# A float32 decoder trunk on one core: plain products for one K-tile pair in four, a two-pass up projection over two blocks at once, and operand work queued in stages

## The chip, the core and the metric

One core of a Trainium2 chip. The metric is the device time of the whole program in microseconds (us), the median of several runs; lower is better.

## The reference, cut to what matters

Two pre-norm residual layers over 256 tokens of width 2048, all in float32. Each layer has a mixer (attention of several kinds between an input and an output projection) and then a squared-ReLU MLP with 8192 hidden columns. The change lies in the MLP.

```
def squared_relu_mlp(h, w_up, w_down):
    return jnp.square(jax.nn.relu(h @ w_up)) @ w_down

for layer in range(2):
    x = x + mixer(rms_norm(x, attn_norm[layer]))
    h = rms_norm(x, mlp_norm[layer])
    x = x + squared_relu_mlp(h, w_up[layer], w_down[layer])
return rms_norm(x, final_norm)
```

## The kernel before, in words

**Three passes for a float32 product.** Each operand is split in two parts of a narrower format: `hi`, the rounded value, which ScalarE writes, and `lo`, the rest, which VectorE gets by a subtraction. A product is then hi·hi + hi·lo + lo·hi. The activations are kept as one tile `xs` per K-tile with the hi columns 0 to 255 and the lo columns 256 to 511; the weights are split as they arrive.

**The stream.** The program is one list, `stream`, of pairs (block, chunk). A block is a set of output columns with its accumulators in PSUM; a chunk is a piece of K, four K-tiles of 128 rows by 256 columns, one `hi` and one `lo` tile of 128x1024. Two or four chunks share a *unit*, 1 MB of weights in a `raw` tile, of which there are three; SyncE loads them in order, each as soon as the last reader of the `raw` tile three units back is done. The loop at the end of `trunk` does for every i: the `hi` tiles up to chunk i+4 (L1265), the `lo` tiles up to chunk i+3 (L1273), then the matmuls of chunk i, and what a finished block needs. Every engine works through its own instructions in this written order. `jobs.tick()` after some chunks takes the next step of the spawned jobs: each job is a generator, and what stands between two of its `yield` lines is written at one place.

**The MLP.** The 8192 hidden columns are eight groups of 1024. In a group the *up* blocks (kind "U", four of 256 hidden columns, four chunks each) make h = relu(x·w_up)^2. The chunks are here called U0 to U15. For each K-tile and 128 columns there are three matmuls of 256 columns (L466 to L468), the first two with the same weights. A finished block (`up_done`) is read from PSUM by ScalarE's Relu (L1003) and squared (L1005), and a job then makes the operands of the next step from the squares `hr`: four additions on VectorE (L1014 to L1017), the hi part on ScalarE (L1018), the lo part on VectorE (L1019).

The *down* projection of groups 0 to 6 uses a product scheme that replaces eight block products of a 2x2 split by seven (kind "S"): four column blocks (`cb`) of 512 columns, each with two units of two K-tile pairs. A unit has four chunks: `plain` (two panels), `single` (one panel), and two whose weights are made on VectorE first, `w13` by L1046 and `w24` by L1052 and L1053. The seven sums of a column block lie in PSUM tiles `s0` and `s1`, are copied out by ScalarE (L1075) and added up in DRAM by GpSimd's accumulating DMAs (L1080). After group 6 `combine` puts the seven sums together in DRAM with seven more accumulating DMAs (L1092) and loads the result (L1096).

Group 0's up chunks stand alone. Then the list has, for each later group, two S chunks of the group before, one up chunk, and so on: `plain`, `single`, U, `w13`, `w24`, U. One *period* is one S unit and two up chunks; a group has eight. The last group's down projection (eight blocks of kind "U") follows, and takes the combined sums in by matmuls with the identity (L1106, `add_sums`).

PSUM: the up blocks have two tiles of one bank each; `s0` and `s1` have two banks each; a separate pool keeps two banks for small side work (`side()`).

## Time and profile before

| | |
|---|---|
| median of 3 runs | 2212.97 us (2207.54 to 2217.98) |
| the profiled execution | 2218.0 us; its span is 2216.2 us |
| TensorE matmul busy | 2160.6 us (97%), 16390 matmuls |
| VectorE busy | 1707.8 us (77%) |
| ScalarE busy | 1297.2 us (59%) |
| DMA | 459.75 MB, mean 207 GB/s |

"Busy" counts an engine as busy while any of its instructions runs, and matmuls overlap each other, so TensorE's 97% is no measure of its pace: the pace is read from the starts of matmuls. "L466" is line 466 of the kernel before; PE is TensorE, DVE VectorE, ACT ScalarE, POOL GpSimd, SPq SyncE's DMA queue. Released waits are written "waiter <- releaser".

### The profile page before, as it was taken

The numbers are of one execution on the slowest core, as the hardware profiler recorded it, in microseconds if no ns is written. First come the engines' busy times: TensorE is split into PE (matmuls) and PEld (weight loads), VectorE is DVE, ScalarE is ACT, GpSimd is POOL, SyncE is SP. The second block draws the span as 40 slices with busy tenths as digits, with TensorE's granted clock in tenths as the row PEclk, the third lists the DMA queues.
The fourth block names the chain that finished last, engine by engine and source line by source line (L and its number), as shares of the span: only waits on it lengthen the run. The fifth ranks groups of instructions, "written<-read, shape, count | busy, mean of one in ns | idle before, by whom it ended". The sixth has DMA issues, their size and how long they took to land.

```text
span 2216.2 us, 40047 instructions
## 1 busy us (share of the span) xinstructions
PE 2160.6 (97%) x16390; PEld 2071.6 (93%) x16390; DVE 1707.8 (77%) x2169; ACT 1297.2 (59%) x1746; POOL 170.7 (8%) x225
## 2 busy tenths in 40 slices
PE   9999999999999999998999999999999999999988
PEld 7898989999999999998988899899999999999987
DVE  6765666888889898886766665568888888889865
ACT  6554545576666666665555446455666666666552
POOL 0000000000000000013100000000000000000131
PEclk9999999999999999999999999999999999999999
DMA  8545456577888888899754455565778888888994
GB/s 261 175 148 162 153 183 179 187 242 222 234 230 233 232 229 234 224 243 263 211 171 141 155 173 179 149 191 178 243 216 237 226 232 232 224 237 232 243 262 135
DMA packets 306279, 459.75 MB, mean 207 GB/s; under 512 B 11992, under 2 KB 181024, under 8 KB 306096
## 3 DMA queue, kind: packets, MB, share of 16 engines
q1 hardware_dynamic: 280224, 392.32, 56.5%
q0 software_dynamic: 25840, 64.87, 14.9%
q8 instruction: 129, 2.11, 0.4%
q14 instruction: 54, 0.44, 0.1%
q10 hardware_dynamic: 32, 0.01, 0.0%
HBM read 403.68 MB, written 60.82 MB: 210 GB/s over the span
## 4 chain that ended last, share of the span: by engine, by line
PE 45%; DVE 17%; ACT 16%; DMA 13%; issue 9%; POOL 1%; ACTq 0%; SPq 0%; DVEq 0%; POOLq 0%
PE mm L475 14%; DVE lo L1273 9%; ACT hi L1265 8%; PE mm L476 8%; DMA raw<-w_up 7%; DVE w L1046 4%; PE up L468 3%; ACT stage L1075 3%; PE up L466 3%; DMA sums<-sums 3%; PE up L467 3%; PE mm L460 2%; DMA raw<-w_down 2%; PE mm L462 2%; PE mm L461 2%
## 5 line engine op out<-in xcount | busy, mean ns | idle before, releaser
L1273 DVE TENSOR_TENSOR lo<-raw,hi 128x1024 fp32r<-128x1024 f32 (+1 forms) x756 | 825.3, 1114 | 242.8 <-ACT hi L1265 83.7
L1265 ACT ACTIVATE hi<-raw 128x1024 fp32r<-128x1024 f32 (+1 forms) x756 | 717.7, 967 | 498.4 <-DMA raw<-w_up 232.9
L468 PE MATMUL up<-xs,lo 128*128 128x256 f32 x2048 | 583.1, 285 | 30.2 <-DVE lo L1273 29.8
L466 PE MATMUL up<-xs,hi 128*128 128x256 f32 x2048 | 580.3, 283 | 8.9 <-ACT hi L1265 7.3
L467 PE MATMUL up<-xs,hi 128*128 128x256 f32 x2048 | 580.2, 283 | 0.0
L499 PE MATMUL s<-hi,hs 128*128 128x256 f32 x1568 | 441.0, 281 | 0.0
L500 PE MATMUL s<-lo,hs 128*128 128x256 f32 x1568 | 440.2, 281 | 0.0
L501 PE MATMUL s<-hi,hs 128*128 128x256 f32 x1568 | 439.8, 280 | 0.0
L468 PEld LDWEIGHTS up<-xs,lo 128*128 128x128 f32 x2048 | 389.7, 190 | 41.6 <-DVE lo L1273 41.6
L466 PEld LDWEIGHTS up<-xs,hi 128*128 128x128 f32 x2048 | 386.8, 189 | 10.0 <-ACT hi L1265 10.0
L467 PEld LDWEIGHTS up<-xs,hi 128*128 128x128 f32 x2048 | 387.0, 189 | 0.0
L475 PE MATMUL mm<-xs,hi 128*128 128x512 f32 x885 | 319.5, 401 | 1.5 <-DVE t L1115 0.9
L1265 ACT ACTIVATE hi<-w 128x1024 fp32r<-128x1024 f32 x224 | 236.1, 1054 | 124.8 <-DVE w L1053 86.7
L500 PEld LDWEIGHTS s<-lo,hs 128*128 128x128 f32 x1568 | 296.0, 189 | 0.0
L499 PEld LDWEIGHTS s<-hi,hs 128*128 128x128 f32 x1568 | 295.6, 189 | 0.0
L501 PEld LDWEIGHTS s<-hi,hs 128*128 128x128 f32 x1568 | 295.4, 188 | 0.0
L1273 DVE TENSOR_TENSOR lo<-w,hi 128x1024 fp32r<-128x1024 f32 x224 | 273.8, 1222 | 21.5 <-ACT hi L1265 16.7
L476 PE MATMUL mm<-xs,lo 128*128 128x256 f32 x944 | 259.0, 279 | 0.2 <-DVE lo L1273 0.2
L475 PEld LDWEIGHTS mm<-xs,hi 128*128 128x128 f32 x885 | 166.0, 188 | 39.2 <-ACT hi L1265 1.1
L476 PEld LDWEIGHTS mm<-xs,lo 128*128 128x128 f32 x944 | 177.3, 188 | 3.0 <-DVE lo L1273 0.5
L1080 POOL DMA_DIRECT2D sums<-stage x96 | 86.6, 902 | 877.3 <-ACT stage L1075 865.7
L1046 DVE TENSOR_TENSOR w<-raw 128x1024 f32<-128x1024 f32 x112 | 136.7, 1220 | 0.0
(295 smaller groups left out, 2775.2 us busy)
## 6 DMA issues: line engine op xcount, KB each, us to landing
raw<-w_up SPq DMA_DIRECT2D x128, 1024.0 KB, 6.0
raw<-w_down SPq DMA_DIRECT2D x128, 1024.0 KB, 6.8
raw<-od_w_in SPq DMA_DIRECT2D x36, 1024.0 KB, 5.0
raw<-ev_w_in SPq DMA_DIRECT2D x30, 1024.0 KB, 5.3
sums<-stage POOLq DMA_DIRECT2D x56, 512.0 KB, 5.8
sums<-stage POOLq DMA_DIRECT2D x56, 384.0 KB, 6.5
raw<-ev_w_out SPq DMA_DIRECT2D x16, 1024.0 KB, 5.0
raw<-od_w_in SPq DMA_DIRECT2D x20, 512.0 KB, 4.7
```

The source lines that it names most:

```text
L466: mm(ps[:, j], hi[:, n, c], m[:, 0:T], start=first and j == 0, stop=False)
L467: mm(ps[:, j], hi[:, n, c], m[:, T:], start=False, stop=False)
L468: mm(ps[:, j], lo[:, n, c], m[:, 0:T], start=False, stop=last and j == 1)
L475: mm(ps[:, j], hi[:, n, c], m, start=first, stop=False)
L476: mm(ps[:, j, 0:T], lo[:, n, c], m[:, 0:T], start=False, stop=False)
L499: mm(ps, x[:, a, 0:P], hi[:, o, q], start=first and at % 2 == 0, stop=False)
L500: mm(ps, x[:, a, 0:P], lo[:, o, q], start=False, stop=False)
L501: mm(ps, x[:, a, P:], hi[:, o, q], start=False, stop=last and (at % 2 == 1 or prod == 3))
L1046: tt(four(t), w[:, :, :, 1].rearrange("p q k c -> p k q c"), w[:, :, 0].rearrange("p q h c -> p h q c"), op=OP.subtract)
L1080: nc.gpsimd.dma_start(to, stage, accum_op=OP.add)
L1265: act(d, r, AF.Copy)
L1273: tt(d, r, f32(h), op=OP.subtract)
```

## The change

1. **Up projection.** A block is now of kind "T", as in the mixers: for each K-tile and 128 columns one matmul of 512 columns (hi weights with hi and lo activations) and one of 256 (lo weights). The products hi·lo come out in PSUM columns of their own, so a block takes two tiles of two banks, and `up_done` becomes: ScalarE copies one half out, VectorE adds the other half to it, ScalarE does Relu and Square. Two blocks that share a 512-column load are worked through together, chunk by chunk: blocks 0 and 1 end at U6 and U7, blocks 2 and 3 at U14 and U15.
2. **One K-tile pair in four without products** (`PLAIN = (3,)`): for pair 3 the eight plain block products replace the seven. It needs no sums of weights and no four additions on `hr`. The sums become eight, in two equal halves of 128x1024; `combine` has one DMA more.
3. **Stages.** `w13` is made when the unit's first `hi` is written, `w24` at its second; the chunk order is `plain`, `single`, `w13`, `w24` as before. The job on `hr` has a `yield` after the additions and one after the hi part; its first step comes with the next tick for blocks 0 and 2 (`delay=b % 2`).
4. **PSUM.** The side pool is gone; in the mixers the side tiles come from the same pool as the other banks, in the MLP `side()` takes half of `s0` or `s1`.

```
@@ consume @@
-                mm(ps[:, j], hi[:, n, c], m[:, 0:T], start=first and j == 0, stop=False)
-                mm(ps[:, j], hi[:, n, c], m[:, T:], start=False, stop=False)
-                mm(ps[:, j], lo[:, n, c], m[:, 0:T], start=False, stop=last and j == 1)
+                o = ps[:, j, 0:T]
...
@@ mlp @@
+        PLAIN = (3,)
...
-        sums = [dram.tile([P, 7 * T], F32, name=f"sums{layer}_{cb}") for cb in range(4)]
+        sums = [dram.tile([P, 8 * T], F32, name=f"sums{layer}_{cb}") for cb in range(4)]
...
         def take_up():
-            return st["banks"].tile([P, 2, T], F32, name="up", bufs=2)
+            return banks("up", 2)
...
         def up_done(grp, b):
             def f(ps):
                 t = temp()
-                act(t, ps, AF.Relu)
+                act(t, ps[:, :, T:], AF.Copy)
+                tt(t, ps[:, :, 0:T], t, op=OP.add)
+                act(t, t, AF.Relu)
+                if (grp, b) != (0, 0):
+                    need(("h", layer) + (grp, b - 1) if b else ("h", layer, grp - 1, nb - 1))
...
+                    elif b in PLAIN:
+                        act(h[:, 0:4, 0:P], r[:, 0:4], AF.Copy)
+                        yield 1, 0
+                        tt(h[:, 0:4, P:], r[:, 0:4], f32(h[:, 0:4, 0:P]), op=OP.subtract)
                     else:
...
                         tt(r[:, 7], r[:, 3], r[:, 5], op=OP.subtract)
+                        yield 1, 0
                         act(h[:, :, 0:P], r[:, 1:8], AF.Copy)
+                        yield 1, 0
                         tt(h[:, :, P:], r[:, 1:8], f32(h[:, :, 0:P]), op=OP.subtract)
...
-                jobs.spawn(job(), keys=[("h", layer, grp, b)], delay=1)
+                jobs.spawn(job(), keys=[("h", layer, grp, b)], delay=b % 2)
...
@@ product_chunks @@
-                chunks += [Chunk(unit, ks, plain, prods=((X11, 1), (X12, 2))),
-                           Chunk(unit, ks, single, prods=((S4, 3),)),
-                           Chunk(unit, ks, of(13), prep13, ((S1, 5), (S3, 7))),
-                           Chunk(unit, ks, of(24), prep24, ((S2, 6), (X22, 4)))]
+                for q in range(2):
+                    if q in prod:
+                        one += [(2 * q, X11, prs[q], 1), (2 * q + 1, X12, prs[q], 2)]
+                    else:
+                        one += [(2 * q, 1, prs[q], 2), (2 * q + 1, 3, prs[q], 2),
+                                (2 * q, 0, prs[q], 4), (2 * q + 1, 2, prs[q], 4)]
...
+                chunks += [Chunk(unit, prs, views_of((4, column)), prep13 if nq else None, one),
+                           Chunk(unit, prs, views_of(*rest), prep24 if nq else None, two)]
...
@@ combine @@
-            for step in (((p2, p1), (p6, p1)), ((p7, p6),), ((p6, p5), (p4, p7)), ((p3, p6), (p7, p5))):
+            for step in (((p2, p1), (p6, p1)), ((p7, p6),), ((p6, p5), (p4, p7), (p8, p5)), ((p3, p6), (p7, p8))):
...
@@ up_list @@
-            blocks = [Block("U", eights(up, grp * W + b * T, KT), mov, up_done(grp, b), take=take_up)
-                      for b in range(nb)]
-            return [(block, i) for block in blocks for i in range(len(block.chunks))]
+            order = []
+            for b in range(0, nb, 2):
+                c = w_chunks(up, grp * W + b * T, fours(KT))
+                two = [Block("T", c[i], mov, up_done(grp, b + i), take=take_up) for i in range(2)]
+                order += [(block, i) for i in range(len(c[0])) for block in two]
+            return order
...
@@ hi_to @@
+            for d, r in views(i, his[i]):
+                act(d, r, AF.Copy)
             prep = stream[i][0].chunks[stream[i][1]].prep
             if prep:
                 prep()
-            for d, r in views(i, his[i]):
-                act(d, r, AF.Copy)
```

**Place 1: VectorE where an up block has ended.** Before, a block's last chunk is followed by two S chunks before the job's turn; `lo_6180` and `lo_6197` are those of `w13` and `w24`, `lo_6216` that of the up chunk behind them.

```order
L1273 TENSOR_TENSOR lo_6180<-w13_6142,hi_6141 128x1024
L1273 TENSOR_TENSOR lo_6197<-w24_6176,hi_6175 128x1024
L1014 TENSOR_TENSOR hr_6173<-hr_6173 128x128
L1015 TENSOR_TENSOR hr_6173<-hr_6173 128x128
L1016 TENSOR_TENSOR hr_6173<-hr_6173 128x128
L1017 TENSOR_TENSOR hr_6173<-hr_6173 128x128
L1019 TENSOR_TENSOR hs_6207<-hr_6173,hs_6207 128x7x128
L1273 TENSOR_TENSOR lo_6216<-raw_6065,hi_6195 128x1024
```

Now, at the end of block 2 of a group (chunk U14, tile `up_5407`); `lo_5762` is that of U15, `lo_5798` and `lo_5808` those of the next S unit's first and second chunk.

```order
L1318 TENSOR_TENSOR lo_5762<-raw_5622,hi_5734 128x1024
L1010 TENSOR_TENSOR t_5782<-up_5407,t_5782 128x512
L1028 TENSOR_TENSOR hr_5786<-hr_5786 128x128
L1029 TENSOR_TENSOR hr_5786<-hr_5786 128x128
L1030 TENSOR_TENSOR hr_5786<-hr_5786 128x128
L1031 TENSOR_TENSOR hr_5786<-hr_5786 128x128
L1067 TENSOR_TENSOR w24_5795<-w13_5760,raw_5636 128x512
L1068 TENSOR_TENSOR w24_5795<-raw_5636,w24_5795 128x512
L1318 TENSOR_TENSOR lo_5798<-raw_5636,hi_5758 128x1024
L1318 TENSOR_TENSOR lo_5808<-raw_5636,hi_5793 128x512
L1318 TENSOR_TENSOR lo_5822<-raw_5738,hi_5806 128x1024
```

The addition from PSUM (L1010) and the four on `hr` (L1028 to L1031) now stand between the `lo` of U15 and the next `lo`, with ScalarE's Relu and Square between L1010 and L1028. On TensorE the twelve matmuls of the unit's two `w` chunks and the sixteen of U15 stand between the end of `up_5407` and the first use of `lo_5798`. The lo part of `hs` (L1035) now comes later, after the next block's addition.

**Place 2: VectorE over one S unit, where the `raw` tile has its last reader.** Before (`raw_6080` is the unit, `raw_6199` the up unit beside it):

```order
L1273 TENSOR_TENSOR lo_6247<-raw_6080,hi_6214 128x1024
L1273 TENSOR_TENSOR lo_6264<-raw_6080,hi_6245 128x512
L1046 TENSOR_TENSOR w13_6279<-raw_6080 128x1024
L1273 TENSOR_TENSOR lo_6282<-raw_6199,hi_6262 128x1024
L1052 TENSOR_TENSOR w24_6309<-w13_6279,raw_6080 128x512
L1053 TENSOR_TENSOR w24_6309<-raw_6080,w24_6309 128x512
```

Now (`raw_5884` is the unit, `raw_5868` and `raw_5989` the up units before and beside it):

```order
L1059 TENSOR_TENSOR w13_6011<-raw_5884 128x1024
L1318 TENSOR_TENSOR lo_6013<-raw_5868,hi_5985 128x1024
L1067 TENSOR_TENSOR w24_6035<-w13_6011,raw_5884 128x512
L1068 TENSOR_TENSOR w24_6035<-raw_5884,w24_6035 128x512
L1318 TENSOR_TENSOR lo_6038<-raw_5884,hi_6009 128x1024
L1318 TENSOR_TENSOR lo_6048<-raw_5884,hi_6033 128x512
L1318 TENSOR_TENSOR lo_6061<-raw_5989,hi_6046 128x1024
```

The last reader of an S unit's `raw` tile was L1053, behind the `lo` of the up chunk beside it; it is now the second `lo` (here `lo_6048`), ahead of that up chunk's `lo`.

## Rows read from the trace of the kernel before

**Rows 1.** Windows, layer 0: stretch, its length, busy us (instructions) by engine, PEclk, DMA share, GB/s.
```profile
407.00:975.00 568.00, 555.77 (x4612) 550.90 (x4611) 503.20 (x584) 371.57 (x433) 42.47 (x52) 1.00 0.81 230
975.00:1038.00 63.00, 56.62 (x441) 55.57 (x441) 46.72 (x47) 37.42 (x45) 23.68 (x31) 0.95 0.97 250
```
**Rows 2.** Waits of PE, 407 to 975 us, then 1512 to 2090 us: total, times, longest.
```profile
PE up L468 <- DVE lo L1273: 12.1, 23, 1.2
...
PE up L468 <- DVE lo L1273: 13.9, 25, 1.4
```
**Rows 3.** The chain of waits, 583 to 612 us: start, us, what.
```profile
585.64 8.79 DMA raw<-w_up
...
595.60 1.23 DVE lo L1273
596.83 0.61 DVE w L1052
...
597.46 0.70 DVE w L1053
...
608.03 9.35 DMA raw<-w_up
```
**Rows 4.** Timeline of PE, single matmuls (up, then S): start us, us, what.
```profile
361.14 0.28 PE L466 MATMUL up<-xs,hi 128*128 128x256 f32 x1
...
445.47 0.28 PE L499 MATMUL s<-hi,hs 128*128 128x256 f32 x1
...
448.32 0.28 PE L466 MATMUL up<-xs,hi 128*128 128x256 f32 x1
...
1037.79 0.28 PE L466 MATMUL up<-hs,hi 128*128 128x256 f32 x1
...
1505.89 0.28 PE L466 MATMUL up<-xs,hi 128*128 128x256 f32 x1
...
1512.01 0.28 PE L466 MATMUL up<-xs,hi 128*128 128x256 f32 x1
```
**Rows 5.** Timeline of PE in the odd mixer, kind "T", six pairs apart.
```profile
1272.15 0.39 PE L475 MATMUL mm<-xs,hi 128*128 128x512 f32 x1
...
1274.25 0.39 PE L475 MATMUL mm<-xs,hi 128*128 128x512 f32 x1
```
**Rows 6.** Groups by line and shape: count, busy us, mean ns, idle before.
```profile
L1005 ACT ACTIVATE hr<-t 128x512 f32<-128x512 f32 x64 | 40.6, 635 | 2.0
L1003 ACT ACTIVATE t<-up 128x512 f32<-128x512 f32 x64 | 37.7, 590 | 16.3 <-PE up L468 16.2
...
L1115 DVE TENSOR_TENSOR t<-up,rB 128x512 f32<-128x512 f32 x15 | 10.4, 691 | 25.0 <-PE up L468 25.0
```
**Rows 7.** Timeline of DVE, the job on `hr` from 588 us.
```profile
588.13 0.28 DVE L1014 TENSOR_TENSOR hr<-hr 128x128 f32<-128x128 f32 x1
...
588.85 0.29 DVE L1017 TENSOR_TENSOR hr<-hr 128x128 f32<-128x128 f32 x1
```
**Rows 8.** Timeline of PE: waits before a fall of the clock, and one without.
```profile
1466.65 0.36 PE L466 MATMUL up<-xs,hi 128*128 128x256 f32 x1 [1.60 <-DVE xT L760]
...
2149.30 0.38 PE L466 MATMUL up<-hs,hi 128*128 128x256 f32 x1 [1.51 <-ACT hs L166]
2150.03 0.38 PE L467 MATMUL up<-hs,hi 128*128 128x256 f32 x1 [0.34 <-DVE hs L167]
```
**Rows 9.** Windows behind that fall (columns of rows 1).
```profile
2151.00:2153.00 2.00, 2.00 (x13) 2.00 (x12) 1.25 (x3) 1.06 (x1) 2.00 (x4) 0.56 1.10 364
2153.00:2155.00 2.00, 2.00 (x13) 2.00 (x12) 1.38 (x2) 0.00 (x0) 0.99 (x2) 0.59 1.25 203
```
**Rows 10.** The page, part 3: queue, kind: packets, MB, share of 16 engines.
```profile
q0 software_dynamic: 25840, 64.87, 14.9%
```
**Rows 11.** Timelines of POOL and PE at the end of layer 1: last sums loaded, first used.
```profile
2186.41 1.63 POOL L1096 DMA_DIRECT2D sum<-sums x3 [2.36 <-DMA sums<-sums]
...
2191.21 1.05 PE L1106 MATMUL up<-misc,sum 128*128 128x128 f32 x8
```

More of the change, by code (lines that the diff above doesn't have):

```diff
@@ L495, in consume_products @@
             ps = block.ps[half].rearrange("p b c -> p (b c)")[:, at * T:(at + 1) * T]
-            for q, pr in enumerate(chunk.kts):
-                x = block.mov(pr)
-                first, last = block.count < 4 and q == 0, block.count >= block.total - 4 and q == 1
-                mm(ps, x[:, a, 0:P], hi[:, o, q], start=first and at % 2 == 0, stop=False)
-                mm(ps, x[:, a, 0:P], lo[:, o, q], start=False, stop=False)
-                mm(ps, x[:, a, P:], hi[:, o, q], start=False, stop=last and (at % 2 == 1 or prod == 3))
+            bank = [(c, n) for c, ch in enumerate(block.chunks) for n, pd in enumerate(ch.prods)
+                    if HOME[pd[3]][0] == half and HOME[pd[3]][1] // 2 == at // 2]
+            x, w = block.mov(pr), slice(m * T, (m + 1) * T)
+            mm(ps, x[:, a, 0:P], hi[:, w], start=(i, o) == bank[0], stop=False)
+            mm(ps, x[:, a, 0:P], lo[:, w], start=False, stop=False)
+            mm(ps, x[:, a, P:], hi[:, w], start=False, stop=(i, o) == bank[-1])
         block.count += 1
@@ L977, in open_pool, with free_half @@
             open_banks(pool_ctx, f"mlp{layer}_ps")
+            turn = [0]
+            def free_half():
+                turn[0] ^= 1
+                return banks(f"s{turn[0]}", 1)[:, 0]
+            st["side"] = free_half
             E["pool"] = pool_ctx.enter_context(tc.tile_pool(name=f"mlp{layer}", bufs=1, reuse_waits="tile"))
@@ L1038, in blocks, with prep13 @@
                     return raw.rearrange("p (q k h c) -> p q k h c", q=2, k=2, c=T)
-                def four(t):
-                    return t.rearrange("p (o q c) -> p o q c", o=2, q=2)
-                def prep13(unit=unit, made=made):
+                def prep13(unit=unit, made=made, nq=sum(a // 2 + q not in PLAIN for q in range(2))):
                     w = blocks(unit.raw)
-                    t = made[13] = E["pool"].tile([P, 1024], F32, name="w13")
-                    tt(four(t), w[:, :, :, 1].rearrange("p q k c -> p k q c"),
-                       w[:, :, 0].rearrange("p q h c -> p h q c"), op=OP.subtract)
@@ L1049, in prep24 @@
-                def prep24(unit=unit, made=made):
+                    t = made[13] = E["pool"].tile([P, 1024], F32, name="w13")[:, 0:2 * nq * T]
+                    tt(t.rearrange("p (o q c) -> p o q c", o=2, q=nq), w[:, 0:nq, :, 1].rearrange("p q k c -> p k q c"),
+                       w[:, 0:nq, 0].rearrange("p q h c -> p h q c"), op=OP.subtract)
+                def prep24(unit=unit, made=made, nq=sum(a // 2 + q not in PLAIN for q in range(2))):
                     w = blocks(unit.raw)
-                    t = made[24] = E["pool"].tile([P, 1024], F32, name="w24")
-                    tt(four(t)[:, 0], four(made[13])[:, 1], w[:, :, 0, 0], op=OP.add)
-                    tt(four(t)[:, 1], w[:, :, 1, 0], four(t)[:, 0], op=OP.subtract)
@@ new lines, in column @@
+                def column(w):
+                    return w[:, :, :, 0].rearrange("p q k c -> p (q k) c")
+                prs = [a // 2, a // 2 + 1]
+                prod = [q for q in range(2) if prs[q] not in PLAIN]
+                plain = [q for q in range(2) if prs[q] in PLAIN]
+                nq = len(prod)
+                one, two, three, four_ = [], [], [], []
+                for q in range(2):
[4 more added lines that the diff above has]
+                                (2 * q, 0, prs[q], 4), (2 * q + 1, 2, prs[q], 4)]
@@ new lines, in product_chunks, with made_views @@
+                if nq:
+                    def made_views(name, made=made, nq=nq):
+                        return lambda raw, dst: [(dst[:, 0:2 * nq * T], made[name])]
+                    for i, q in enumerate(prod):
+                        three += [(i, S1, prs[q], 5), (nq + i, S3, prs[q], 7)]
+                        four_ += [(i, S2, prs[q], 6), (nq + i, X22, prs[q], 4)]
+                    chunks += [Chunk(unit, prs, made_views(13), prods=three),
+                               Chunk(unit, prs, made_views(24), prods=four_)]
@@ L1198, in last_block @@
             act(sq[:, j], xl[:, j], AF.Square)
-        sums, turn = banks("s0", 1), side()
+        sums, turn = banks("s1", 1), side()
         def add_up(a, first, last):
```

62 lines of the change are left out of this document (38 added, 24 removed).

## The prediction

> **What bounds the kernel now.** I read the windows by stage first, then who waits for whom, then the chain of waits, and last single matmuls for TensorE's pace.
>
> The change lies in the two MLPs. In the stretch where up and S chunks alternate, TensorE is busy 556 of 568 us, VectorE 503, and the DMA engines have a share of 0.81; in the last 63 us, where the sums are combined, the DMA share is 0.97 [rows 1]. So TensorE sets the pace and is held up now and then. By whom: nearly every wait of PE is for a `lo` at L468 [rows 2].
>
> How much in all comes from the pace. An up triple starts every 0.360 us (17 triples from 1505.89 to 1512.01), an S matmul every 0.1188 us (24 from 445.47 to 448.32) [rows 4]. Group 0 has 128 triples, 46.1 us; a later group 336 S matmuls and 128 triples, 39.9 + 46.1 = 86.0 us; 46.1 + 7 × 86.0 = 648.0 us. Layer 0 took 676.65 us from its first up matmul to its first down matmul [rows 4]. So 28.7 us are lost. The waits listed are 12.1 us in 23 pieces (layer 1: 13.9 in 25) [rows 2]; a matmul is drawn 0.28 us long but one starts every 0.12, so each hides 0.16 more: 15.8 and 17.9 us. The other 12.9 us of layer 0 lie in the last stretch, where DMA is full.
>
> Why `lo` is late shows in the chain of waits [rows 3]: a load of w_up is issued at 585.64 and lands 8.79 us later; then `hi`, `lo`, L1052 and L1053 in turn free the S unit's tile, and the load two periods on goes out at 608.03. That is 22.39 us for two periods in which TensorE has work for 2 × (42 × 0.1188 + 16 × 0.360) = 21.5. It is a loop of latencies: a load cannot start before VectorE has passed the `lo` of the up chunk that came with the load before.
>
> **The change part by part.**
>
> *Up matmuls.* 2048 triples become 2048 pairs of 512 and 256 columns. In the odd mixer, where such pairs run now, six take 2.10 us, 0.350 each [rows 5], against 0.360: 2048 × 0.0095 = **−19.5 us**. The Trainium skill ("TensorE: Matmul & The Clock Gate", Back-to-back issue gap) gives a lone matmul's gap as its columns at 2.4 GHz plus 2.5 ns, which as an estimate makes a triple 327.5 ns and a pair 325.0. By it the saving would be 5.1 us and my result 14 us later; both paces measured here are higher than that, and the rows decide.
>
> *Plain products.* Eight instead of seven for one pair in four: three more matmuls × 4 column blocks × 7 groups × 2 layers = 168 × 0.1188 = **+20.0 us**. The two edits cancel on TensorE.
>
> *The loop of loads.* An S unit's tile is now free after its second `lo`, ahead of the up chunk's `lo` (place 2), so the w_up load no longer hangs on the one before. VectorE has less to do as well: pair 3 needs no sums. I take the waits of the alternating stretch as gone: **−33.7 us** (15.8 + 17.9); bounds 0 (late loads of w_down take over) and −33.7.
>
> *The end of a block.* This is where I expect a new wait (place 1). For blocks 0 and 2, VectorE's next `lo` now stands behind the PSUM addition and the four additions on `hr`, and these behind ScalarE's Relu and Square. Nothing of it can start before TensorE has ended the block. From there: ScalarE's copy 0.59, VectorE's addition 0.69 (row of L1115, which also reads `up`), Relu and Square 0.635 each [rows 6], the four additions 1.0 (588.13 to 589.14) [rows 7], `w24` 1.33, `lo` 1.23 [rows 3], and some 0.4 for six hand-overs: 6.5 us. TensorE meanwhile has 12 S matmuls (1.43), eight pairs (2.80) and the next chunk's first matmul (0.12): 4.35 us. It waits 2.15 us, for each even block, twice a group. Block 1's own `hr` additions (1.0) come before another `lo` that has no more than a quarter of a microsecond to spare; I take 0.75 once a group, between 0 and 1.0. Groups 1 to 6 of both layers: 12 × (2 × 2.15 + 0.75) = **+60.6 us**. In group 0 three up chunks (8.4 us) cover the chain; group 7 falls in the stretch with full DMA, below. Behind the waiting addition on VectorE stand all later `lo`; ScalarE's Relu waits in turn, with the next `hi` behind it, but these are four chunks ahead. The lower bound is 0, if TensorE comes late to these places anyway, the upper the rival with the clock below.
>
> The old job held VectorE up too (hi part of `hs` on ScalarE, between its additions and its lo part); that wait goes, and its price is in the 33.7.
>
> *The sums.* Each column block moves 128 KB more out of PSUM and has one accumulating DMA more. GpSimd's queue takes 14.9% of 2216.2 us for 64.87 MB [rows 10], 5.1 us per MB: 0.26 MB × 5.1 = 1.3 us per column block. Where DMA is full this is time: three blocks × 2 layers × 1.3 = 8 us, and group 7's waits lie in the same stretch and give DMA time; I take **+4**, bounds 0 and 8. At the end of layer 1 the last sums are issued until 2188.0 and first used at 2191.2 [rows 11], so nothing is to spare, and four more DMAs in a queue that waits for each step make them later by about 1 us each; TensorE's own extra time hides half: **+2**, bounds 0 and 6. Before group 7 all this lies beside matmuls and costs nothing.
>
> *Small.* The added copy, addition and Relu of 64 blocks cost nothing beyond the chain above: ScalarE is busy 372 of 568 us [rows 1]. Loading w_up in longer rows I take as nothing, since loads are not short of rate but late; SyncE's order of loads, S and up in turn, stays. The PSUM pools: layer 1's first up matmul waits 1.6 us for a bank now [rows 8]; with other banks it may or may not, ±1.6, taken as 0.
>
> Sum: −19.5 + 20.0 − 33.7 + 60.6 + 4 + 2 = **+33.4 us**. The profiled execution took 2218.0 us, 5 above the median of 2213.0; 2251.4 against it, and **2246 us** as a median.
>
> **The rivals.**
>
> *The clock falls at the new waits.* The granted clock was 0.56 and 0.59, half speed for most of four microseconds, from 2151 to 2155 [rows 9], after two waits drawn 1.51 and 0.34 long, 2.3 us with what the drawing hides (0.16 and 0.26); after 1.60, really 1.76, at 1466.65 it stayed at full speed [rows 8]. A wait of 2.15 lies between. The fall cost (0.44 + 0.41) × 2 = 1.7 us. 24 waits × 1.7 = 41, less the 0.75 that a slower TensorE absorbs (12 × 0.75 = 9): 2278 us. For it: the nearness to 2.3. Against: one unbroken wait of this length does not occur in the trace, and most waits of the alternating stretch leave its clock at 1.00 [rows 1].
>
> *The loop was the whole matter, and the end of a block is covered* (faster). Place: `lo_5798`. Price: all but the 60.6: 2213 − 27 = 2186 us. It decides if the chain takes at most 4.35 us instead of 6.5, or TensorE has 2.15 us more to do there. For it: waits of PE are put down to `lo` today with a VectorE that is behind, and the change empties VectorE. Against: each link of the chain waits for the one before, and the chain starts at TensorE's own end of block, so an emptier VectorE does not shorten it.
>
> *Part and part* (no change). The waits at the end of a block come, but half as long (1.1 us and no second one, 26 us): 2213 − 1 = 2212 us. It needs Relu and Square to overlap or `w24` to be passed earlier.
>
> *The merged matmul saves nothing.* Pairs would keep the pace of triples, 0.360: 19.5 us more, 2266. For it: nothing in the trace, since the mixers' pairs run in the same mix of engines [rows 5]; chance 0.04, counted with the clock's case, whose times it shares. The rule of the skill named above lies near this one.
>
> **How the numbers follow.** Forecast, slower by the new waits (2225 to 2262, its own range): 0.42. With the clock, or without a saving on matmuls (2262 to 2294): 0.15. Part and part (2202 to 2224): 0.18. Faster (2170 to 2202): 0.25. A measurement of this kernel can tell about 0.5%, 11 us, from no change, so slower is 0.57, same 0.18, faster 0.25. The range 2182 to 2276 us leaves out half of the clock's case and a third of the faster one, some 0.15.
>
> **What would show it.** In the profile after: waits of PE for a `lo` at a hi·lo matmul of S, about 2 us long, two per group, each right behind a block's U chunk, and hardly any at an up chunk's 256-column matmul; DMA as a releaser of `hi` nearly gone; S matmuls 4872; up pairs 0.350 us apart; in the last stretch of each layer DMA share still near 1. PEclk below 1.0 in the alternating stretch would speak for the clock. I am wrong if PE's waits there are under 1 us, or if the loads of w_down now hold `w13` up and PE waits in every period.

## The result, and the profile after

The changed kernel takes 2276.4 us (median of four runs, 2271.0 to 2278.6) beside 2214.2 of the kernel before: ratio 1.0281, interval 1.0248 to 1.0313. Slower was right. The size was not: 62 us instead of 33, just above the top of the range, 2276. The profiled execution took 2271.0 us, its span is 2269.2; against the profiled execution of before (2218.0) that is 53 us, and these are followed here. The other nine lie between executions: the profiled one of before is the slowest of its four, that of after the fastest of its four.

Who waits for whom, TensorE's rows (waiter <- releaser: us in total, times, longest):

```profile
PE s L498 <- DVE lo L1318: 52.9, 28, 2.2
PE up L1148 <- DMA sum<-sums: 10.8, 3, 4.9
PE up L469 <- DVE lo L1318: 3.3, 2, 2.5
PE up L477 <- DVE lo L1318: 3.0, 4, 0.8
```

In [rows 2] the waits for `lo` lay at the third matmul of an up triple (L468), 23 and 25 to a layer. Now there are 28 at an S matmul, two for each of seven groups in two layers. One of them among the single matmuls, with what follows (start, us, engine, line, operation, [idle before]):

```profile
499.38 0.28 PE L497 MATMUL s<-hi,hs 128*128 128x256 f32 x1
501.56 0.38 PE L498 MATMUL s<-lo,hs 128*128 128x256 f32 x1 [1.90 <-DVE lo L1318]
501.78 0.28 PE L499 MATMUL s<-hi,hs 128*128 128x256 f32 x1
502.96 0.35 PE L497 MATMUL s<-hi,hs 128*128 128x256 f32 x1
503.10 0.42 PE L498 MATMUL s<-lo,hs 128*128 128x256 f32 x1
503.32 0.42 PE L499 MATMUL s<-hi,hs 128*128 128x256 f32 x1
```

From 499.38 to 501.56 is 2.18 us where 0.12 is the pace: a wait of 2.06. One and a half microseconds later the matmuls start 0.21 us apart instead of 0.12. The windows (PEclk is the third number from the right) say why:

```profile
407.00:975.00 568.00, 540.68 (x3701) 499.19 (x3700) 448.14 (x591) 372.50 (x471) 38.84 (x48) 0.98 0.77 223
502.00:504.00 2.00, 2.00 (x16) 2.00 (x15) 2.00 (x4) 0.77 (x3) 0.00 (x0) 0.76 0.87 274
504.00:506.00 2.00, 2.00 (x8) 1.71 (x8) 1.98 (x2) 1.57 (x3) 0.00 (x0) 0.50 0.95 286
```

The clock falls to half after the wait, which costs 0.24 x 2 + 0.50 x 2 = 1.5 us. By the single matmuls this follows 13 of the 28 waits, 0.2 to 1.5 us after their end. The length alone does not tell which: of the 24 waits that are drawn 1.90 long, 11 are followed by a fall; the first of each layer (1.42) is not, the last of each (2.24 and 2.23) is. The mean over the stretch is 0.98, where it was 1.00 [rows 1]. What VectorE and ScalarE do ahead of that wait is the forecast's chain, in order of time:

```profile
495.34 0.60 ACT L1009 ACTIVATE t<-up 128x512 f32<-128x512 f32 x1 [0.84 <-PE up L479]
495.97 0.69 DVE L1010 TENSOR_TENSOR t<-up,t 128x512 f32<-128x512 f32 x1 [2.26 <-ACT t L1009]
496.69 0.63 ACT L1011 ACTIVATE t<-t 128x512 f32<-128x512 f32 x1 [0.76 <-DVE t L1010]
497.36 0.63 ACT L1015 ACTIVATE hr<-t 128x512 f32<-128x512 f32 x1
498.02 0.29 DVE L1028 TENSOR_TENSOR hr<-hr 128x128 f32<-128x128 f32 x1 [1.36 <-ACT hr L1015]
498.96 0.68 DVE L1067 TENSOR_TENSOR w<-w,raw 128x512 f32<-128x512 f32 x1
500.29 2.95 DVE L1318 TENSOR_TENSOR lo<-raw,hi 128x1024 fp32r<-128x1024 f32 x3
```

The stage marks (first up, first S and first down matmul and the next mixer of layer 0; first S and first down of layer 1):

```profile
362.08 0.40 PE L476 MATMUL up<-xs,hi 128*128 128x512 f32 x1
407.85 0.28 PE L497 MATMUL s<-hi,hs 128*128 128x256 f32 x1
1055.09 0.28 PE L467 MATMUL up<-hs,hi 128*128 128x256 f32 x1
1122.61 0.40 PE L476 MATMUL mm<-xs,hi 128*128 128x512 f32 x1
1543.05 0.28 PE L497 MATMUL s<-hi,hs 128*128 128x256 f32 x1
2188.40 0.28 PE L467 MATMUL up<-hs,hi 128*128 128x256 f32 x1
```

The same marks of before, as far as [rows 4] does not have them, and last the last transposes of before and of after:

```profile
407.87 0.28 PE L499 MATMUL s<-hi,hs 128*128 128x256 f32 x1
1092.02 0.47 PE L475 MATMUL mm<-xs,hi 128*128 128x512 f32 x1 [0.88 <-DVE t L1115]
1513.44 0.28 PE L499 MATMUL s<-hi,hs 128*128 128x256 f32 x1
2142.42 0.28 PE L466 MATMUL up<-hs,hi 128*128 128x256 f32 x1
2206.05 0.67 PE L1207 MATMUL side<-misc,xT 128*128 128x128 f32 x2
2259.25 0.42 PE L1252 MATMUL s<-misc,xT 128*128 128x128 f32 x2
```

So the 53 us divide (us; the last stage runs to the last transposes):

| stretch | before | after | difference |
|---|---|---|---|
| up and S alternating, layer 0 / 1 | 629.9 / 629.0 | 647.2 / 645.4 | +17.3 / +16.4 |
| down stage, layer 0 / 1 | 54.2 / 63.6 | 67.5 / 70.9 | +13.3 / +7.2 |
| group 0, both layers; mixers | 93.5; 735.8 | 91.6; 736.7 | -1.9; +0.9 |

At their paces the matmuls of the alternating stretch take 7 x (348 x 0.1188 + 128 x 0.350) = 603 us a layer. So 86.6 us are lost there in the two layers: 57.4 at the 28 waits (52.9 drawn and 0.16 hidden in each), 4.0 at the four of 0.8, 13 x 1.5 = 19.5 to the clock, and some 6 in small delays that I did not follow.

### The profile page after: what moved, and what is told of

It is laid out like the page before. It is cut to its first block, busy times and chain, and to the rows that moved or that the text cites. A ratio compares the mean times of both kernels' runs of the same rounds, so it can differ in the third digit from the quotient of the medians.

```text
span 2269.2 us, 36534 instructions
## 1 busy us (share of the span) xinstructions
PE 2178.9 (96%) x14510; PEld 1995.5 (88%) x14510; DVE 1624.1 (72%) x2233; ACT 1327.1 (58%) x1866; POOL 176.7 (8%) x233
## 4 chain that ended last, share of the span: by engine, by line
issue 48%; PE 37%; DMA 9%; POOL 4%; ACT 1%; DVE 1%; POOLq 0%; SPq 0%; ACTq 0%
PE mm L476 14%; DMA sums<-sums 8%; PE mm L477 8%; POOL sums L1120 3%; PE up L476 3%; PE mm L460 2%; PE mm L461 2%; PE mm L462 2%; PE up L477 1%; PE mm L479 1%; PE side L351 1%; DMA sums<-stage 1%; PE side L374 1%; PE side L420 1%; POOL sum L1138 1%
## 5 line engine op out<-in xcount | busy, mean ns | idle before, releaser
L1307 ACT ACTIVATE hi<-raw 128x1024 fp32r<-128x1024 f32 (+2 forms) x812 | 737.0, 929 | 494.2 <-PE mm L476 106.3
L1318 DVE TENSOR_TENSOR lo<-raw,hi 128x1024 fp32r<-128x1024 f32 (+2 forms) x812 | 843.5, 1064 | 219.3 <-PE mm L477 74.8
L476 PE MATMUL up<-xs,hi 128*128 128x512 f32 x1920 | 696.9, 400 | 1.6 <-DVE xT L758 1.6
L498 PE MATMUL s<-lo,hs 128*128 128x256 f32 x1624 | 463.4, 285 | 53.0 <-DVE lo L1318 52.9
L499 PE MATMUL s<-hi,hs 128*128 128x256 f32 x1624 | 460.6, 284 | 0.0
L497 PE MATMUL s<-hi,hs 128*128 128x256 f32 x1624 | 459.7, 283 | 0.0
L476 PEld LDWEIGHTS up<-xs,hi 128*128 128x128 f32 x1920 | 366.9, 191 | 79.4 <-ACT hi L1307 1.9
L498 PEld LDWEIGHTS s<-lo,hs 128*128 128x128 f32 x1624 | 310.0, 191 | 63.5 <-DVE lo L1318 62.2
L1318 DVE TENSOR_TENSOR lo<-w,hi 128x1024 fp32r<-128x1024 f32 x224 | 212.0, 955 | 97.1 <-PE up L477 43.0
L1307 ACT ACTIVATE hi<-w 128x1024 fp32r<-128x1024 f32 x224 | 187.0, 837 | 72.5 <-ACT hi L1307 27.2
L1115 ACT ACTIVATE stage<-s 128x1024 f32<-128x1024 f32 x112 | 113.9, 1017 | 39.1 <-PE s L499 39.1
L1059 DVE TENSOR_TENSOR w<-raw 128x1024 f32<-128x1024 f32 x112 | 106.5, 951 | 2.2 <-DMA raw<-w_down 2.2
L1010 DVE TENSOR_TENSOR t<-up,t 128x512 f32<-128x512 f32 x64 | 44.0, 687 | 75.0 <-ACT t L1009 74.7
```

Source lines behind the costliest of these rows:

```text
L476: mm(ps[:, j], hi[:, n, c], m, start=first, stop=False)
L497: mm(ps, x[:, a, 0:P], hi[:, w], start=(i, o) == bank[0], stop=False)
L498: mm(ps, x[:, a, 0:P], lo[:, w], start=False, stop=False)
L499: mm(ps, x[:, a, P:], hi[:, w], start=False, stop=(i, o) == bank[-1])
L1059: tt(t.rearrange("p (o q c) -> p o q c", o=2, q=nq), w[:, 0:nq, :, 1].rearrange("p q k c -> p k q c"), w[:, 0:nq, 0].rearrange("p q h c -> ...
L1115: act(stage, ps.rearrange("p b c -> p (b c)"), AF.Copy)
```

## The experiments

Each ran beside the kernel before, whose medians there were 2213 to 2218 us; where a time is set against the changed kernel, that is 2276. A difference of a few microseconds from 2276 is within the intervals, so it is read from the stretches of the traces and not from the time.

**The four additions later.**

```diff
-                jobs.spawn(job(), keys=[("h", layer, grp, b)], delay=b % 2)
+                jobs.spawn(job(), keys=[("h", layer, grp, b)], delay=1)
```

> The changed kernel with the first step of the job on hr one tick later for blocks 0 and 2 too (delay=1), so that VectorE's four additions stand behind w24 and the next lo instead of ahead of them. My theory (a chain of hand-overs at the end of a block makes that lo late, and the waits pull the clock down): the 28 waits of 2.06 us go (58 us), the slow matmuls they bring go too (some 13 us); 2276 - 71 = 2205 us, PEclk 1.00 in the alternating stretch, and what the down stages lost (some 20 us) stays. Rival, VectorE is simply full there: the waits move to the lo behind the additions, about 1.0 us each, 28 us, 2235 us. Rival, late loads take over once VectorE is early: ACT waits for raw again and PE for lo at up chunks, over 2225 us.

Measured 2272.6 us (ratio 1.0262, 1.0234 to 1.0290). TensorE's waits:

```profile
PE s L498 <- DVE lo L1318: 39.7, 26, 1.6
PE up L477 <- DVE lo L1318: 14.0, 16, 0.9
```

A miss. The wait at 499.4 is gone, and another of 1.55 us stands at 504.55, behind the end of the second block: its Square must wait until the first block's `hr` has been used up, and so the steps that were put off pile up there. In all 53.7 us of waits for `lo`, beside 55.9 without the edit. PEclk is 1.00 over the stretch; the alternating stretches are 3.9 and 2.1 us shorter, the down stage of layer 0 is 5.9 longer.

**The hi products of an S chunk first.**

```diff
             mm(ps, x[:, a, 0:P], hi[:, w], start=(i, o) == bank[0], stop=False)
-            mm(ps, x[:, a, 0:P], lo[:, w], start=False, stop=False)
-            mm(ps, x[:, a, P:], hi[:, w], start=False, stop=(i, o) == bank[-1])
+            mm(ps, x[:, a, P:], hi[:, w], start=False, stop=False)
+            late.append((ps, x[:, a, 0:P], w, (i, o) == bank[-1]))
+        for ps, xh, w, last in late:
+            mm(ps, xh, lo[:, w], start=False, stop=last)
```

> The changed kernel with the matmuls of each S chunk in another order: all products with the hi weights first, then those with lo. Nothing else moves. TensorE has 7 more matmuls (0.83 us) before it needs the late lo. My theory: each of the 28 waits becomes 1.23 us instead of 2.06 (-23 us), and the clock falls after fewer of them, up to 13 us more: 2240 to 2253 us. If the wait were not for lo: 2276 us. If the clock's falls do not hang on the length of the wait: 2253 us with as many slow stretches as now.

Measured 2267.5 us (1.0238, 1.0211 to 1.0264). The 28 waits are 1.07 us long as drawn, but 28 stand at an up chunk 8 to 9 us later (23.0 us, where there were four and 3.0 us): again 52.8 us in all. PEclk is 1.00 over the stretch; the alternating stretches are 6.1 and 3.8 us shorter, the down stages 5.8 and 2.6 longer. Cover at one place is no cover when VectorE is late for the next place too.

**Matmuls in the gap.**

```diff
+            for _ in range(17 if block.ends and (i, o) == (0, 0) else 0):
+                mm(ps, x[:, a, 0:P], hi[:, w], start=False, stop=False)
             mm(ps, x[:, a, 0:P], lo[:, w], start=False, stop=False)
```

> The changed kernel with 17 copies of a matmul (0.119 us each, 2.02 us) put ahead of the first matmul that needs the late lo, at 26 of the 28 places (not in the first S chunk of a layer); they add the same product 17 more times to the accumulator, so the output is not the reference's. TensorE then works through the gap, but gains nothing in time by it. Theory that the wait itself makes the clock fall: the waits vanish from the list, PEclk is 1.00 in the alternating stretch, and the time falls by the slow matmuls alone, some 13 us: 2263 us. Rival, the clock falls for another reason (the load of the chip as a whole): slow matmuls as now, 2276 us. If the extra matmuls hold up others or draw the clock down themselves: above 2276 us.

Measured 2272.1 us (1.0260, 1.0227 to 1.0293). Over the alternating stretch, and TensorE's waits at up chunks in the whole run:

```profile
407.00:975.00 568.00, 561.80 (x3946) 521.83 (x3945) 453.23 (x598) 375.42 (x474) 38.94 (x48) 1.00 0.78 226
PE up L477 <- DVE lo L1322: 10.4, 14, 0.8
```

With TensorE at work in the gap its clock does not fall, so the wait is what lowers it. The alternating stretches are 6.0 and 3.4 us shorter; the down stages were 6.2 and 4.0 us longer, which hides it in the sum. The 9.4 us are only half of the 19.5 that the falls cost, because the second wait is back: 14 times, where there were 4 and 3.0 us. In the changed kernel a TensorE at half clock came late to ten of these places and had no wait there. So the clock's price, net of that, is some 10 us.

**The stages alone, in the kernel before.**

```diff
-                chunks += [Chunk(unit, ks, plain, prods=((X11, 1), (X12, 2))),
-                           Chunk(unit, ks, single, prods=((S4, 3),)),
-                           Chunk(unit, ks, of(13), prep13, ((S1, 5), (S3, 7))),
-                           Chunk(unit, ks, of(24), prep24, ((S2, 6), (X22, 4)))]
+                chunks += [Chunk(unit, ks, plain, prep13, ((X11, 1), (X12, 2))),
+                           Chunk(unit, ks, single, prep24, ((S4, 3),)),
+                           Chunk(unit, ks, of(13), prods=((S1, 5), (S3, 7))),
+                           Chunk(unit, ks, of(24), prods=((S2, 6), (X22, 4)))]
...
+                        yield 1, 0
                         act(h[:, :, 0:P], r[:, 1:8], AF.Copy)
+                        yield 1, 0
```

> The kernel before with the third part of the change alone: w13 made at the unit's first hi and w24 at its second, prep behind the hi, and a yield in the job on hr after the additions and one after the hi part; blocks, products, PSUM and the delay of the job stay. Theory of the loop of loads: an S unit's tile is free two chunks earlier, the waits of the alternating stretch go, 2214 - 33.7 = 2180 us, and ACT hardly waits for raw of w_up. Rival, the loop is only moved (VectorE does the same work, and the load of w_up hangs on another lo): 2205 to 2214 us. Rival, an earlier w24 blocks VectorE for a late load of w_down: slower than 2214 us.

Measured 2175.3 us (0.9827, 0.9800 to 0.9855). The alternating stretch, and its last part, which ends at 1010.6 here:

```profile
407.00:975.00 568.00, 568.00 (x4762) 568.00 (x4761) 513.01 (x602) 394.53 (x449) 49.03 (x60) 1.00 0.87 237
947.60:1010.60 63.00, 62.24 (x521) 61.95 (x520) 50.87 (x52) 39.55 (x47) 20.79 (x27) 1.00 1.02 273
```

TensorE works all 568 us, and no wait for `lo` above 0.8 us is left. The stretches fall by 27.4 and 26.8 us to 602.6 and 602.1, which is their matmuls' pace (602.0). That is more than the 33.7 I had given the loop of loads: the 12.9 us of the last part, where the DMA share is now 1.02, went as well, so they were not the full DMA's. That they were the loop's is argued: the edit also moves the steps of the job on `hr`, and ScalarE still waits 133.5 us for loads of w_up (232.9 before), where I expected hardly any. What each of the two is worth was not separated. The down stages give back 9.3 and 0.8 us.

**The emptying of an up block put off whole.**

```diff
             def f(ps):
-                t = temp()
-                act(t, ps[:, :, T:], AF.Copy)
...
                 def job():
+                    t = temp()
+                    act(t, ps[:, :, T:], AF.Copy)
+                    tt(t, ps[:, :, 0:T], t, op=OP.add)
...
+                    yield 1, 0
...
-                jobs.spawn(job(), keys=[("h", layer, grp, b)], delay=b % 2)
+                jobs.spawn(job(), keys=[("h", layer, grp, b)], delay=1)
```

> The changed kernel with the whole emptying of an up block (ScalarE's copy, VectorE's addition, Relu, Square) moved into the job and one tick later, then the four additions one tick after that. After the earlier runs (the waits only moved when the additions moved, or when TensorE came later) my theory is that VectorE loses time standing in the chain ScalarE, VectorE, ScalarE, VectorE with every lo behind it, and that any place inside it only shifts the wait. Deferred, the addition meets a block that is long done. Expected: waits of PE for lo under 10 us a layer, the alternating stretch at its matmuls' pace, 7 x (348 x 0.1188 + 128 x 0.350) = 603 us instead of 647 and 645, of which the down stages give back some 6 us each since the sums in GpSimd's queue then come later against TensorE: 2276 - 86 + 12 = 2202 us. Rival, VectorE has no room whatever the order: waits of 25 us or more a layer remain somewhere else, 2255 to 2276 us.

Measured 2226.4 us (1.0041, 1.0026 to 1.0056), 50 less than the changed kernel. TensorE's waits, 407 to 2150 us:

```profile
PE up L477 <- DVE lo L1318: 18.2, 26, 1.0
PE up L467 <- DVE t L1011: 13.9, 2, 9.4
```

Waits for `lo` fall from 55.9 to 19.7 us (18.2 in 26 and 1.5 in 2), under the theory's 10 a layer. The stretches fall to 622.8 and 627.7, which is 20 and 25 us above their pace. Of these, 4.5 and 9.4 are the one wait for L1011 at the end of each stretch: the edit makes the last block's own addition late. So the chain was most of the matter, and some 12 us a layer of waits for `lo`, with what the drawing hides, stay.

**Triples again, two blocks at once kept.**

```diff
-                act(t, ps[:, :, T:], AF.Copy)
-                tt(t, ps[:, :, 0:T], t, op=OP.add)
-                act(t, t, AF.Relu)
+                act(t, ps[:, :, 0:T], AF.Relu)
...
-                two = [Block("T", c[i], mov, up_done(grp, b + i), take=take_up) for i in range(2)]
+                two = [Block("U", c[i], mov, up_done(grp, b + i), take=take_up) for i in range(2)]
```

> The changed kernel with the up blocks of two at once kept, but with three matmuls of 256 columns for each K-tile and the old emptying of the bank (one Relu on ScalarE, no copy, no addition on VectorE). My theory: matmuls take 0.0095 x 2048 = 19.5 us more; the chain at the end of a block loses copy, addition and two hand-overs, 1.5 us, so 28 waits of 2.06 become 0.6 (-41 us) and the clock stays up (-10): 2276 + 19.5 - 51 = 2245 us. Rival, the waits go altogether because VectorE no longer stands between two steps of ScalarE: 2230 us. Rival, the waits come from the order of the stages and not from the addition: 2295 us. If pairs save nothing against triples, each of these is 19.5 us lower.

Measured 2244.7 us (1.0122, 1.0107 to 1.0137). That the theory's 2245 is met is luck in part: the alternating stretches are 22.4 and 21.3 us shorter, more than it had, and the down stages 11.3 and 7.8 longer, which it left out. The S waits are 12.6 us in 26, 0.5 each as drawn. The chain has lost ScalarE's copy, VectorE's addition and two hand-overs, and that takes two thirds of the wait.

**No plain products.**

```diff
-        PLAIN = (3,)
+        PLAIN = ()
```

with seven sums and seven DMAs in `combine` as before.

> The changed kernel without plain products (no pair in PLAIN): seven products for all pairs, seven sums, combine with seven DMAs. Theory: 168 matmuls fewer, 168 x 0.1188 = -20 us, the waits at the end of blocks as now, and GpSimd's chain shorter by a step's wait, -6 us: 2250 us. Rival, VectorE's added work (w13 and w24 for pair 3, four additions on hr) comes back as waits for lo: 2265 to 2285 us. If nothing of the matmuls is seen because TensorE waits anyway: 2276 us.

Measured 2233.5 us (1.0066, 1.0049 to 1.0083): 43 less, not 26. Waits for `lo` at S and up chunks are 52.6 us, beside 55.9, but in 56 pieces instead of 32 and none above 1.4 us; the clock stays at 1.00, and the down stages are 4.3 and 6.5 us shorter. VectorE's added work did come back as waits, 36.2 us of them at up chunks, but in pieces after which the clock did not fall.

**The added sum in the first step of combine.**

```diff
-            for step in (((p2, p1), (p6, p1)), ((p7, p6),), ((p6, p5), (p4, p7), (p8, p5)), ((p3, p6), (p7, p8))):
+            for step in (((p2, p1), (p6, p1), (p8, p5)), ((p7, p6),), ((p6, p5), (p4, p7)), ((p3, p6), (p7, p8))):
```

> The changed kernel with the added accumulating DMA of combine (p8 += p5) in the first step instead of the third, so that the last step (p7 += p8) doesn't wait for it. Theory for the 20 us that the down stages lost: GpSimd's queue takes one column block's chain after the other, 26 us each before and 28 to 30 after, longer than TensorE needs for a column block, so that the added wait of 2 to 3 us adds up over four blocks and TensorE waits for the last sums. Expected: PE waits for sums gone or below 3 us in all, down stages shorter by 5 to 8 us each, 2276 - 13 = 2263 us. Rival, the last stretch is short of DMA rate and the added 128 KB cost what they cost wherever they stand: 2274 to 2278 us.

Measured 2273.0 us (1.0250, 1.0233 to 1.0267); the down stages are 69.2 and 74.1 us, no shorter. My theory of the one added wait fell; its rival, DMA rate, fits this run, and the next one decides. First GpSimd's queue for the last column block of layer 0, after:

```profile
1057.87 1.00 ACT L1115 ACTIVATE stage<-s 128x1024 f32<-128x1024 f32 x1
1067.63 1.83 POOL L1120 DMA_DIRECT2D sums<-stage  x1
1082.13 1.75 POOL L1134 DMA_DIRECT2D sums<-sums  x2
1090.16 0.80 POOL L1134 DMA_DIRECT2D sums<-sums  x1 [6.27 <-DMA sums<-sums]
1094.17 2.47 POOL L1134 DMA_DIRECT2D sums<-sums  x3 [3.21 <-DMA sums<-sums]
1107.08 1.65 POOL L1138 DMA_DIRECT2D sum<-sums  x3 [3.85 <-DMA sums<-sums]
```

and before:

```profile
1036.01 1.01 ACT L1075 ACTIVATE stage<-s 128x1024 f32<-128x1024 f32 x1
1037.31 1.28 POOL L1080 DMA_DIRECT2D sums<-stage  x1
1052.21 1.76 POOL L1092 DMA_DIRECT2D sums<-sums  x2
1072.84 1.65 POOL L1096 DMA_DIRECT2D sum<-sums  x3 [3.83 <-DMA sums<-sums]
```

The copy of the last sums out of PSUM ends at 1058.9, and GpSimd issues their DMA at 1067.6, since it still stands in the chain of the column block before; in the kernel before it was there 0.3 us after the copy. In ten kernels the down stage of layer 0 follows the issue of those last loads, counted from its first matmul:

| kernel | loads at | stage |
|---|---|---|
| before | 35.1 | 54.2 |
| no plain products | 45.5 | 63.2 |
| stages alone | 46.0 | 63.5 |
| after | 52.0 | 67.5 |
| emptying put off | 52.5 | 68.1 |
| added sum first | 52.8 | 69.2 |
| additions later / hi first / filler | 56.9 / 57.1 / 57.4 | 73.4 / 73.3 / 73.7 |
| triples | 62.7 | 78.8 |

**The sums on VectorE.** The sums of a column block are loaded at once and added in on-chip memory; no DMA waits for another. To make room, the `hs` tiles of pair 3 have four panels instead of seven.

```diff
-            for step in (((p2, p1), (p6, p1)), ((p7, p6),), ((p6, p5), (p4, p7), (p8, p5)), ((p3, p6), (p7, p8))):
-                for to, src in step:
-                    nc.gpsimd.dma_start(to, src, accum_op=OP.add)
-                yield 2, 0
...
+            for i, n in enumerate(names):
+                nc.gpsimd.dma_start(at[n], sums[cb][:, i * T:(i + 1) * T])
+            yield 3, 0
+            for to, src in pairs:
+                tt(at[to], at[to], at[src], op=OP.add)
```

> The changed kernel with the eight sums of a column block put together by VectorE in on-chip memory (eight additions of 128x256 after one step of loads) instead of by eight accumulating DMAs in four steps that wait for each other in GpSimd's queue. Seen so far, over before and five other kernels: the down stage of layer 0 lasts as long as the issue of the last loads of sums after its first matmul, plus some 16 us (45.5 and 63.2, 46.0 and 63.5, 52.0 and 67.5, 52.8 and 69.2, 62.7 and 78.8), but no less than 54. My theory: that chain, and not DMA rate or the sum's size alone, sets the down stage; with it gone the stage falls to some 55 us in layer 0 (from 67.5) and to some 63 in layer 1 (from 70.9), 2276 - 20 = 2256 us; the alternating stretch stays at 645 to 647. Rival, the last stretch is short of DMA rate: the stage stays above 63 us, 2268 us or more. Rival, the additions hold up lo on VectorE: new waits of PE for lo in the down stage, no gain.

Measured 2257.9 us (1.0190, 1.0175 to 1.0205). The down stages are 55.7 and 62.6 us, PE waits for no sums any more, and the stage runs with a DMA share of 0.73:

```profile
1058.00:1114.00 56.00, 54.18 (x451) 53.54 (x450) 48.02 (x72) 31.57 (x45) 11.52 (x23) 1.00 0.73 216
```

The two stages are 11.8 and 8.3 us shorter, so the 20 us were GpSimd's chain. Short of rate the stage was not before either: in the changed kernel the DMA share is 0.81 from 1055 to 1122 us. The alternating stretches grew by 3.1 and 4.5 us, which the expectation did not have. How much of the chain's lateness is the eighth sum and how much the earlier schedule was not separated; a hint is that with seven sums the stages are 63.2 and 64.4 us without plain products and 63.5 and 64.4 with the stages alone.

**Three kernels with the sums on VectorE.** The edits are those above, put together.

> The deferred emptying of the up blocks and the sums on VectorE together. If the two costs are separate and the down stage gives nothing back any more: 2226 - 13 - 8 = 2205 us. If a shorter alternating stretch shows other waits of the down stage (late loads of w_down): 2215 to 2226 us.

> The kernel before with the stages alone, and the seven sums on VectorE. The alternating stretch has no waits left there (0.9 us a layer) and its down stages are 63.5 and 64.4 us. With the chain in GpSimd's queue gone: 2175 - 9 - 2 = 2164 us. If the down stages of that kernel are set by DMA rate: 2175 us.

> Two blocks at once in 512- and 256-column passes, with the emptying deferred, seven products for every pair, and the sums on VectorE. Against the kernel with stages alone it has 2048 x 0.0095 = 19.5 us less of matmuls and more work on ScalarE and VectorE (a copy and an addition for each block). If VectorE has room: waits as with the deferred emptying and plain products (some 18 us a layer), 2205 - 20 = 2185 us, and were they gone too, 2145 us. If VectorE's work for pair 3 (w13, w24, four additions) comes back as waits: 2195 to 2205 us. So the pairs would gain less than their emptying costs in waits, and the stages alone stay ahead.

Emptying put off: 2209.1 us (0.9980, 0.9969 to 0.9991), near the 2205 expected. Stages alone: 2175.5 us (0.9822, 0.9807 to 0.9837), no gain; the down stages fell to 54.2 and 59.7 as expected, but VectorE stood up to 5.6 us for the loads of sums among the S chunks, with `lo` behind it, and the stretches grew to 615.8 and 608.7. Without plain products: 2256.9 us (1.0195, 1.0177 to 1.0214), a miss by far. There TensorE waits 28.0 and 20.9 us for `lo` and 23.1 for the lo part of `hs`. Its clock fell too, 11 times in the two alternating stretches. VectorE is busy 506 of 568 us [as 503 in rows 1], with 448 in the changed kernel. That the plain pair gives VectorE the room that the emptying takes would fit, but is not shown: with the stages alone VectorE is busy 513 us, and TensorE waits for `lo` once, 0.8 us.

**Two open points.** Additions seven ticks after the loads instead of three, in the kernel with stages alone; and two `hr` tiles in the one with the emptying put off. Both give other sums than the reference, for a reason that the traces do not show, so nothing is read of their down stages.

> The kernel before with the stages alone and the seven sums on VectorE, the additions seven ticks after the issue of the loads instead of three. With three, VectorE stood 5.6 us for the loads twice a layer, with lo behind it, and TensorE waited 5.5 us (10.5 us in layer 0, 5.6 us in layer 1, and 5 us of slow matmuls). If that place was all, the alternating stretches fall back to 602 us each and the down stages stay at 54 and 60: 2175 - 13 - 6 = 2156 us. If the additions themselves cost VectorE what TensorE then waits for: 2165 to 2175 us.

> The changed kernel with the emptying deferred, the sums on VectorE (additions seven ticks after the loads), and two hr tiles instead of one, so that the second block's Square no longer forces the first block's last steps into the same place. If the 16 us of waits that the deferral left in each layer come from that forced piling-up: under 5 us of waits a layer, alternating stretches of some 607 us, 2209 - 30 = 2179 us. If they come from what VectorE has to do between two block ends, wherever it stands: 2200 to 2212 us.

2180.9 us (0.9840, 0.9819 to 0.9862) and 2223.0 us (1.0034, 1.0022 to 1.0047). In the first the alternating stretches are 602.0 and 601.4 us without a wait: it was the place. In the second 12.1 and 13.7 us of lost time at waits stay where it was 15.9 and 16.1: it is not the single `hr` tile alone. That it is what VectorE has to do between two block ends is what is left, and not shown.

**The version that beats both.**

```diff
-            yield 3, 0
+            yield (7 if cb < 2 else 3), 0
```

> The kernel before with the stages alone and the seven sums on VectorE, the additions seven ticks after the issue of the loads for the first two column blocks, which lie among S chunks, and three for the last two, which lie in the down stage. If the waits were a matter of place: alternating stretches of 602 us as with seven ticks, down stages of 54 and 60 us as with three, 2175.5 - 13.9 - 7.2 = 2154 us, faster than both kernels. If the additions shift work of VectorE into the down stage: 2160 to 2175 us.

2158.6 us (0.9749, 0.9736 to 0.9762). Its alternating stretches are 602.4 and 601.4 us, its down stages 54.2 and 59.7:

```profile
407.00:975.00 568.00, 568.00 (x4762) 568.00 (x4762) 514.61 (x608) 394.62 (x449) 47.91 (x62) 1.00 0.87 238
```

It has triples, single up blocks and seven products everywhere, as the kernel before.

## Why the prediction was half right

- *Matmuls.* Right: S matmuls are 4872 (3 x 1624), pairs start 0.350 us apart (five starts from 379.96 to 381.36), and group 0 is 0.9 us shorter in each layer, where 128 pairs were to save 1.2. As an estimate from the gap of a lone matmul that the Trainium skill gives ("TensorE: Matmul & The Clock Gate", Back-to-back issue gap) a pair would be 0.325 us; here it is not, and the rows decided.
- *The loop of loads.* Right that it goes, too small in size: 54.2 us with the stages alone, where the forecast took off 33.7. The step that failed is "the other 12.9 us of layer 0 lie in the last stretch, where DMA is full": the place was right, the cause was not, since this time went while the DMA share there rose to 1.02.
- *The end of a block.* Right in place, and near in length: 28 waits of 2.06 where 24 of 2.15 stood in the sum, since group 7 has its two as well, and the second wait 4 times instead of 12, since the clock hid it (with matmuls in the gap it comes 14 times). That 61.4 us came out against 60.6 is in part luck. But "that chain" is not the whole of it: moving one link moved the wait (additions later, hi first). What holds is that VectorE stands in a chain of hand-overs with every `lo` behind it; taking it out of there is worth 50 us (emptying put off).
- *The clock.* I made it a rival with 24 x 1.7 - 9 = 32 us. It came, after 13 of 28 waits, and costs 19.5, some 10 net of the second waits that it hides. Against it I had said that one unbroken wait of this length does not occur in the trace of before. That was misread: it holds two longer ones, and the clock was at half soon after each (the two waits, and a window behind each):

```profile
1026.58 0.39 PE L466 MATMUL up<-xs,hi 128*128 128x256 f32 x1 [2.45 <-ACT hi L1265]
2108.05 0.39 PE L466 MATMUL up<-xs,hi 128*128 128x256 f32 x1 [2.72 <-ACT hi L1265]
1028.50:1030.50 2.00, 2.00 (x12) 2.00 (x11) 1.93 (x3) 1.27 (x2) 0.00 (x0) 0.50 0.93 129
2110.50:2112.50 2.00, 2.00 (x11) 2.00 (x11) 1.93 (x3) 1.80 (x2) 0.00 (x0) 0.50 1.04 160
```

- *The alternating stretch in sum.* Forecast -17.1 + 20.0 - 33.7 + 60.6 = +29.8, measured +33.7. That these are near is luck: the clock and the 6 us not followed, left out of the sum, nearly cancel the mis-sized loop.
- *The sums.* This is the term that failed and that put the time outside the range: +4 and +2, 6 us in all; the down stages measured +13.3 and +7.2, 20.5 in all. I priced four more DMAs by their bytes and by 1 us each at the end. What counts is GpSimd's queue, in order, with four steps that wait for each other. In layer 0 its last loads of a column block come 27 to 30 us apart, where TensorE makes a column block in 24.6 (four copies of `s1`, from 984.1 to 1057.9); each block starts later than the one before it. With the sums on VectorE the 20 us are gone.
- *The signs named.* Waits at S, two per group: yes, and four at up chunks. The DMA share of the last 63 us ahead of the down stage is 0.99. ScalarE's waits for w_up fell from 232.9 to 73.3 us, less than "nearly gone". PEclk below 1.0 did speak for the clock.

## What to carry to other kernels

Several edits were timed as one, and the good one was hidden: of the four parts the stages alone are worth 38 us in the kernel before, and with the other three on top the time is 100 us longer. Before an engine's work is put between two steps of another, look at what stands behind it in its own queue; a late link can be moved, but only a place where nothing has to be waited for frees the queue. And a chain of dependent DMAs has a rate of its own: set it against the time in which the bound engine makes the next item, since a faster kernel will meet it.

## What the runs showed of the hardware

- One wait drawn 1.90 us long (really 2.06) between dense matmuls was followed by a fall of the granted clock to 0.50 in 11 of 24 cases, 0.2 to 1.5 us after its end; with matmuls in the gap the clock stayed at 1.00. Waits of 1.07 and 1.28 us (drawn), nine microseconds apart, and of 1.55 (additions later) left it at 1.00 over the stretch.
- GpSimd stood 1.2 to 6.3 us after a step of accumulating DMAs of 128 KB within DRAM before the next could go out: 28 waits, 102.2 us in the changed kernel.
- A full DMA did not by itself slow TensorE: with the stages alone, the DMA share was 1.02 over the last 63 us ahead of the down stage, and TensorE was busy 62.2 of them.
